# An encoder layer on one core: K and Q convolutions in a lane of their own, scan outputs kept in the keys' tile, masks in their own stream, and a reordered start

## The chip, the cores and the metric

One core of a Trainium2 chip runs the whole layer in one launch. The metric is the device time in microseconds (us); the kernel before has a median of 1962.57 us over 3 runs (1962.05 to 1963.68). PE is the matrix engine, DVE the vector engine, ACT the scalar engine, POOL the general one, SP the engine that issues nearly all DMAs.

## The reference, cut to what matters

```python
h = rmsnorm(h_res, norm1_w)                 # 16 meta tokens + 1024 tokens, 1024 channels
q, k, v, z, beta, a, sc_b, sc_c, sc_x, gate_a, gate_b = split(h @ w_in)
qkv = silu(depthwise_conv5(concat(q, k, v)))
q = l2norm(q) * 128**-0.5 ; k = l2norm(k)   # 8 heads of 128 channels
# per head, forwards and backwards, in chunks: lmat = strict(beta * (k k^T) * decay), (I + lmat)^-1, then
#   v_new = u - w S ; o = q exp(g) S + (q k^T * decay) v_new ; S = S exp(g_last) + k_dec^T v_new
o = rmsnorm(o_fwd + o_bwd) * dn_norm_w * silu(z)
merged = sigmoid(gate_a) * (o @ w_bdn) + sigmoid(gate_b) * ((sc_b * conv3(sc_c * sc_x)) @ w_bsc)
h_res += merged @ w_out ; h_res += swiglu(rmsnorm(h_res, norm2_w)) @ w_down ; out = rmsnorm(h_res)
```

## The kernel before, in words

All large products split each fp32 operand into a high and a low fp32r part and add three products (high by high, high by low, low by high); in `dense_steps` (L332) one step is these three matmuls for one of eight 128-row pieces of the weight.

**The start (L989 to L1172).** Nine row tiles `xs[t]` of the input are loaded. `root(t)` squares a tile on ACT and takes the inverse root on POOL; `scaled(t)` multiplies on DVE by the root and by `w1row`, the norm weight on all 128 partitions (one 512 KB DMA on SP, L1070); `turned(t)` transposes on PE into two PSUM banks; `highs(t)` writes the high parts `hTh` on ACT, `lows(t, g)` the low parts `al` on DVE. `keep_warm(n)` is n transposes of the identity whose result nothing reads. `gen0` and `gen1` are the generators of the first two weight units, K and Q of head 0; `u0` and `u1` are their weights, the high part cast on ACT, the low part subtracted on POOL. `rows` holds the convolution taps, which two transposes turn into `wc` and `cols`; `wba` are the 32 columns of beta and a, used by `small_gates`.

**Phase 1 (L1303 to L1325).** A Python planner writes the order of all engines by hand. It takes 128-column weight units one after another (24 units of K, Q and V, 8 of z, 24 of the short convolution, 7 of the gates; 9 gate units are left to phase 2, `LATE`), and after each dense step it calls `run_streams()` and `pump()`. Streams are generators that emit the small work of a head: `g_gates` (once), `g_decay` (the decay factors `PQ`), `g_norm` (norms and the K K^T and Q K^T products), `g_inv` (the triangular inverse) and `g_scan` (the two scans of a head and its output). `pump` fills DVE with jobs from lanes: the convolutions, the forward substitution `fs`, small `norm` jobs. Of the lanes that are ready, the one with the least weighted DVE time goes first. `T` holds the planner's clock for each engine; it sets the order only.

**The tiles in question.** `kq` (three buffers) holds a head's keys and queries, [128, 2, 1040]; `NP` and `PQ` (two buffers each) the inverse and the decayed products. The scan accumulates its outputs in `oacc`, views of `NP`; at its end they are scaled on ACT (L893), transposed on PE, multiplied by z on DVE into the other half of `NP` (L899) and stored to `o_d` (L902). `freed` counts scans that have read their `kq` for the last time, `done` scans whose store is issued. K of head h takes a `kq` buffer when `freed` is at least h - 2; its first writer is the ACT copy L389. `g_norm` of head h takes `NP` when the store of head h - 2 is expected to be over.

**Phase 2** (from L1326) is the rest of the layer with seven products for eight blocks; its code is not touched.

## Time and profile before

| what | value |
|---|---|
| median of 3 runs | 1962.57 us (1962.05 to 1963.68) |
| the profiled execution | 1961.08 us, span 1959.4 us |
| granted TensorE clock, mean | 0.999 |
| PE busy | 1941.7 us, 99% of the span, 11962 matmuls |
| DVE, ACT, POOL busy | 1468.1, 867.9, 158.4 us |
| PE idle from 0 to 30 us (the start) | 30.00 - 24.92 = 5.08 us |
| PE idle from 30 to 960 us (phase 1) | 930.00 - 926.09 = 3.91 us |
| PE idle from 960 to 1900 us | 940.00 - 938.31 = 1.69 us |

A stretch's idle time is its length less PE's busy time in it. Matmuls are pipelined and their ends are modelled, so a matmul that waits only shortly still looks busy. The profiled execution is 1.49 us under the median.

### The profile page before, as it was taken

What the parts mean: (1) busy time and instruction counts of PE and PEld (TensorE: products, weight loads), DVE (VectorE), ACT (ScalarE), POOL (GpSimd) and SP (SyncE); (2) the same over time, 40 slices, a digit from 0 to 9 for tenths busy, and PEclk for the clock granted to TensorE, in tenths of its full rate; (3) what the DMA queues carried; (4) which work ended last, traced back from release to release, by engine and by line L of the source; (5) the groups of instructions that cost most, each with busy time, mean ns of one, the idle gap of its engine ahead of it and who ended that gap; (6) DMA issues with size and microseconds to landing.
All of it is one profiled execution on the core that took longest, in us unless ns stands there. A gap on an engine that the chain in (4) does not pass through costs nothing.

```text
span 1959.4 us, 31938 instructions
## 1 busy us (share of the span) xinstructions
PE 1941.7 (99%) x11962; PEld 1704.4 (87%) x11962; DVE 1468.1 (75%) x2804; ACT 867.9 (44%) x2014; POOL 158.4 (8%) x457
## 2 busy tenths in 40 slices
PE   8999999999999999999999999999999999999998
PEld 8998899999899999998888888887888888888887
DVE  4778778788887888787358798559787887756574
ACT  5463544646455554533445545234232332324343
POOL 3012112020110202110000000000000000000001
PEclk9999999999999999999999999999999999999999
DMA  4222332323222222224386623332666644587654
GB/s 146 68 76 80 103 99 60 87 60 87 60 76 67 85 65 79 70 69 153 103 310 246 206 88 121 115 119 73 212 232 209 209 165 163 179 279 243 194 181 155
DMA packets 243136, 264.11 MB, mean 135 GB/s; under 512 B 46820, under 2 KB 166933, under 8 KB 240549
## 3 DMA queue, kind: packets, MB, share of 16 engines
q1 hardware_dynamic: 242981, 262.07, 42.1%
q8 instruction: 94, 1.54, 0.3%
q14 instruction: 61, 0.50, 0.1%
HBM read 189.58 MB, written 72.44 MB: 134 GB/s over the span
## 4 chain that ended last, share of the span: by engine, by line
PE 89%; DVE 5%; ACT 3%; issue 1%; DMA 1%; POOL 0%; SPq 0%; POOLq 0%; DVEq 0%; ACTq 0%
PE pm L332 31%; PE pm L1382 5%; PE pd L1382 4%; PE pe L1382 3%; PE pm L1656 3%; PE pm L1658 3%; PE pm L1657 2%; PE pd L1658 2%; PE pd L1656 2%; PE pd L1657 2%; PE pe L1658 2%; PE pe L1656 2%; PE pe L1657 2%; PE pm L1814 1%; PE pm L1815 1%; PE pm L1813 1%
## 5 line engine op out<-in xcount | busy, mean ns | idle before, releaser
L332 PE MATMUL pm<-hTh,wh 128*128 128x512 f32 (+4 forms) x1328 | 483.8, 365 | 0.1
L332 PE MATMUL pm<-hTh,wl 128*128 128x512 f32 (+4 forms) x1328 | 450.5, 340 | 0.0
L332 PE MATMUL pm<-al,wh 128*128 128x512 f32 (+4 forms) x1328 | 449.6, 339 | 0.5 <-DVE al L1047 0.5
L332 PEld LDWEIGHTS pm<-hTh,wl 128*128 128x128 f32 x1328 | 249.1, 188 | 15.5
L332 PEld LDWEIGHTS pm<-hTh,wh 128*128 128x128 f32 x1328 | 250.2, 189 | 13.6 <-ACT hTh L1041 0.2
L332 PEld LDWEIGHTS pm<-al,wh 128*128 128x128 f32 x1328 | 250.4, 189 | 12.9 <-DVE al L1047 0.7
L87 DVE TENSOR_TENSOR al<-raw,ring_h 128x1024 fp32r<-128x1024 f32 x73 | 88.4, 1223 | 63.6 <-ACT ring_h L86 63.2
L86 ACT CAST ring_h<-raw 128x1024 fp32r<-128x1024 f32 x73 | 76.9, 1054 | 109.7 <-PE pd L1815 35.3
L940 DVE TENSOR_TENSOR wl<-raw,wh 128x512 fp32r<-128x512 f32 x122 | 84.1, 690 | 32.0 <-ACT wh L943 27.1
L355 DVE SCALAR_TENSOR_TENSOR kq<-ra,wc,kq 128x520 f32<-128x520 f32 (+1 forms) x128 | 95.9, 749 | 2.3 <-ACT kq L389 1.2
L821 ACT ACTIVATE w<-pd,small 128x128 f32<-128x128 f32 x128 | 40.2, 365 | 124.9 <-PE pd L814 106.4
L128 POOL TENSOR_SCALAR ss<-ss 128x1 f32<-128x1 f32 x13 | 4.6, 353 | 951.1 <-ACT b L1825 603.4
L491 DVE TENSOR_TENSOR tm<-fP,fN 128x135 f32<-128x135 f32 (+23 forms) x248 | 72.1, 291 | 10.0 <-DMA fN<-nd 3.3
L495 DVE TENSOR_TENSOR fP<-fP,tm 128x135 f32<-128x135 f32 (+23 forms) x248 | 71.8, 289 | 7.3
L943 ACT CAST wh<-raw 128x512 fp32r<-128x512 f32 x122 | 74.8, 619 | 0.1
L87 DVE TENSOR_TENSOR raw<-pair,raw 128x1024 fp32r<-128x1024 f32 (+1 forms) x42 | 48.0, 1143 | 30.4 <-ACT raw L86 30.4
L86 ACT CAST raw<-pair 128x1024 fp32r<-128x1024 f32 (+1 forms) x42 | 41.7, 992 | 58.4 <-PE pd L1382 27.5
L87 DVE TENSOR_TENSOR wl<-pair,wh 128x1024 fp32r<-128x1024 f32 (+1 forms) x42 | 48.1, 1144 | 21.7 <-ACT wh L86 21.6
L86 ACT CAST wh<-pair 128x1024 fp32r<-128x1024 f32 (+1 forms) x42 | 41.7, 992 | 46.0 <-PE pd L1382 24.7
L843 DVE SCALAR_TENSOR_TENSOR S<-S,eGl,pd 128x128 f32<-128x128 f32 x104 | 31.8, 344 | 38.2 <-PE pd L831 30.8
L130 POOL TENSOR_TENSOR small<-small,minus_half 128x9 f32<-128x9 f32 x16 | 29.5, 1842 | 353.8 <-DVE small L878 264.0
L661 POOL TENSOR_TENSOR tm<-mP,mN 1x15 f32<-1x15 f32 (+7 forms) x120 | 37.3, 311 | 237.0 <-DMA mN<-ndm 228.7
(660 smaller groups left out, 4945.7 us busy)
## 6 DMA issues: line engine op xcount, KB each, us to landing
raw<-in_w_in_dram SPq DMA_DIRECT2D x64, 512.0 KB
raw<-in_w_gate_up_dram SPq DMA_DIRECT2D x44, 512.0 KB
sums<-in_w_down_dram SPq DMA_DIRECT2D x22, 512.0 KB
t_d<-sums SPq DMA_DIRECT2D x11, 1024.0 KB
raw<-s_d SPq DMA_DIRECT2D x44, 256.0 KB
raw<-t_d SPq DMA_DIRECT2D x44, 256.0 KB
act_d<-b SPq DMA_DIRECT2D x43, 256.0 KB
raw<-act_d SPq DMA_DIRECT2D x33, 256.0 KB
```

The lines of the kernel that those rows point to most:

```text
L86: nc.scalar.copy(hi, src)
L87: nc.vector.tensor_tensor(out=lo, in0=src, in1=hi.bitcast(F32), op=ALU.subtract)
L332: mm(po[:, :n], (wl if j == 2 else wh)[:, k], xl[k][:, t0:t0 + n] if j == 1 else xh[k][:, t0:t0 + n], start=(i == 0), stop=(i == 3 * KT - 1))
L355: nc.vector.scalar_tensor_tensor(out=acc, in0=raw[:, h0 + t:h0 + t + hn], scalar=wc[:, t, col:col + 1], in1=acc, op0=ALU.mult, op1=ALU.add)
L491: nc.vector.tensor_tensor(out=tv, in0=fP[:, 0:r, j:j + 1].broadcast_to([P, r, n]), in1=fN[:, j:j + 1, j + 1:32].broadcast_to([P, r, n]), o ...
L495: nc.vector.tensor_tensor(out=fP[:, 0:r, j + 1:32], in0=fP[:, 0:r, j + 1:32], in1=tv, op=ALU.subtract)
L940: nc.vector.tensor_tensor(out=u[1][1][:, k], in0=u[2][:, k], in1=u[1][0][:, k].bitcast(F32), op=ALU.subtract)
L943: nc.scalar.copy(u[1][0][:, k], u[2][:, k])
L1382: mm(bank[t], a[:, c], b, start=fresh, stop=first and k == 3 and j == 2, skip_group_check=not first)
L1656: mm(po, ah[:, k], bhk, start=k == 0, stop=False)
L1657: mm(po, ah[:, k], blk, start=False, stop=False)
L1658: mm(po, al[:, k], bhk, start=False, stop=k == 3)
```

## The change

- K and Q convolutions go into a lane `kq` with weight 0.2; V's stay in `conv`, and a ready `conv` job gives way to any other.
- At the end of a scan all eight output tiles are scaled into the keys' half of the head's `kq` (`osc`), then transposed; the product with z goes into the queries' half (`oTs`), and the store reads that. `NP` is given back once the scaling is done (`scaled`), and K of head h waits for `done` instead of `freed`.
- The masks for the meta tokens (`Dm`) leave `g_gates` and become a stream `g_meta`; `g_norm` copies the small product out raw and multiplies by mask and scale in one instruction later.
- The norm weight is loaded as one row of 4 KB from ACT's queue and spread to all partitions by two products with a row of ones (`one_row`) and two DVE copies. 44 identity transposes become 8, the two products, and 24.
- Tiles 0 to 2 are reordered: `scaled(2)` ahead of the high and low parts, the weight's split ahead of `highs(1)`, the second halves of the low parts last, and the transposes of `rows` behind the first sweep of `gen0`.

```diff
-    WEIGHT = {"conv": 1.0, "short": 1.0, "fs": 0.33, "norm": 0.1}
+    WEIGHT = {"kq": 0.2, "conv": 1.0, "short": 1.0, "fs": 0.33, "norm": 0.1}
...
+            if len(cand) > 1 and "conv" in cand:
+                cand.remove("conv")
...
-                    while freed < h - 2:
+                    while done < h - 2:
...
-                job = enqueue("conv", conv_job(raw, dst, col, sub, META if i == 1 else 0))
+                job = enqueue("conv" if i == 2 else "kq", conv_job(raw, dst, col, sub, META if i == 1 else 0))
...
-        nc.vector.tensor_tensor(out=Nm, in0=pt[:META, P:P + META], in1=Dm[:, h], op=ALU.mult)
+        nc.vector.tensor_copy(Nm, pt[:META, P:P + META])
...
-        nc.vector.tensor_scalar(out=Nm, in0=Nm, scalar1=cc[:META, 8, 0:1], scalar2=None, op0=ALU.mult)
+        while not gated:
+            yield T["pe"] + 100
+        nc.vector.scalar_tensor_tensor(out=Nm, in0=Nm, scalar=cc[:META, 8, 0:1], in1=Dm[:, h], op0=ALU.mult, op1=ALU.mult)
         on("dve", 950)
-        while done < h - 1 or "PQ" not in st_:
+        while "PQ" not in st_ or h > 1 and "scaled" not in heads[h - 2]:
             yield T["pe"] + 100
         if h > 1:
-            yield heads[h - 2]["stored"]
+            yield heads[h - 2]["scaled"]
...
+        osc, oTs = (kq[:, a, 0:SEQ].rearrange("p (c t) -> p c t", c=NC) for a in range(2))
+        t = [0, 0]
+        for c in range(NC):
+            nc.scalar.activation(osc[:, c], oacc[c], AF.Copy, scale=y[:, c:c + 1])
+            t[c // 4] = A(P)
+        st_["scaled"] = t[1]
         for c4 in range(2):
-            oT = NP[:, 4 * c4:4 * c4 + 4, 1 - c4]
+            oT = oTs[:, 4 * c4:4 * c4 + 4]
             pt = newbank()
+            yield t[c4]
             for c in range(4):
-                nc.scalar.activation(oacc[4 * c4 + c], oacc[4 * c4 + c], AF.Copy, scale=y[:, 4 * c4 + c:4 * c4 + c + 1])
-                t = A(P)
-            yield t
-            for c in range(4):
-                transpose(pt[:, c], oacc[4 * c4 + c])
+                transpose(pt[:, c], osc[:, 4 * c4 + c])
...
+        if ndec == 1 and not metas and not gated:
+            metas.append([g_meta(), T["dve"] + HOP, None])
...
+        nc.gpsimd.memset(one_row, 1.0)
+        nc.scalar.dma_start(w1row[0:1], norm1_w[0:1, :])
...
-        nc.sync.dma_start(w1row, norm1_w[0:1, :].broadcast_to([P, D]))
...
-        keep_warm(44)
+        keep_warm(8)
+        for c in (slice(0, 512), slice(512, 1024)):
+            pw = psm()
+            mm(pw, one_row, w1row[0:1, c], start=True, stop=True)
+            nc.vector.tensor_copy(w1row[:, c], pw)
+        keep_warm(24)
...
         turned(1)
         root(2)
+        scaled(2)
         highs(0)
         lows(0, 0)
-        scaled(2)
+        nc.scalar.copy(u0[1][0], u0[2])
+        nc.gpsimd.tensor_tensor(out=u0[1][1], in0=u0[2], in1=u0[1][0].bitcast(F32), op=ALU.subtract)
+        keep_warm(4)
+        turned(2)
+        highs(1)
+        lows(1, 0)
+        highs(2)
+        lows(2, 0)
         lows(0, 1)
-        highs(1)
...
         lows(1, 1)
...
         lows(2, 1)
+        root(3)
+        steps(gen0)
         pt = psd()
         transpose(pt[:, :120], rows[:120, 0], 120)
         pt2 = psd()
         transpose(pt2[:, :25], rows[:25, 1], 25)
-        root(3)
-        steps(gen0)
```

The new lines shift the later ones: L332 of before is L334 of the changed kernel, L389 is L391, L893 is L896, L902 is L909.

**First place: PE at the start.** `pm<-ident` are the identity transposes, `xr` the input tiles, `pe<-rows` the taps' transposes, `hTh` and `al` the high and low parts. Before:

```order
L83 MATMUL pm_174<-ident 128x128 x44
L83 MATMUL pd_247<-ident,xr_155 128x128 x4
L83 MATMUL pe_252<-ident,xr_155 128x128 x4
L83 MATMUL pm_174<-ident 128x128 x4
L83 MATMUL pd_266<-ident,xr_156 128x128 x4
L83 MATMUL pe_271<-ident,xr_156 128x128 x4
L83 MATMUL pm_174<-ident 128x128 x6
L83 MATMUL pd_295<-ident,xr_157 128x128 x4
L83 MATMUL pd_300<-ident,xr_157 128x128 x4
L83 MATMUL pe_314<-ident,rows 128x120
L83 MATMUL pe_316<-ident,rows 128x25
L332 MATMUL pm_321<-hTh_129,wh_194 128x336 x4
```

The changed kernel, from tile 2's transposes to the beta and a columns (ahead of it stand 8 identity transposes, the two 512-column products, 24 identity transposes and tiles 0 and 1):

```order
L83 MATMUL pd_286<-ident,xr_160 128x128 x4
L83 MATMUL pm_291<-ident,xr_160 128x128 x4
L334 MATMUL pm_311<-hTh_129,wh_196 128x336 x4
L334 MATMUL pm_311<-hTh_130,wh_196 128x336 x4
L334 MATMUL pm_311<-al_126,wh_196 128x336 x4
L334 MATMUL pm_311<-al_127,wh_196 128x336 x2
L334 MATMUL pm_311<-al_128,wh_196 128x336 x2
L334 MATMUL pm_311<-hTh_129,wl_197 128x336 x4
L334 MATMUL pm_311<-hTh_130,wl_197 128x336 x4
L83 MATMUL pe_336<-ident,rows 128x120
L83 MATMUL pe_338<-ident,rows 128x25
L1065 MATMUL pe_351<-hTh_129,wba 64x336
```

The two transposes of the taps have moved from ahead of the 24 matmuls of the sweep to behind them, directly ahead of the first matmul that needs `wba`.

**Second place: ACT at the start**, from tile 1's high parts on; `jk_first` is the squaring of a tile, `wc` and `cols` read the taps' banks. Before:

```order
L1041 CAST hTh_129<-pd_266 128x4x128
L1041 CAST hTh_130<-pe_271 128x4x128
L1100 CAST wh_194<-raw_180 128x1024
L1041 CAST hTh_129<-pd_295 128x4x128
L1041 CAST hTh_130<-pd_300 128x4x128
L1016 ACTIVATE jk_first,rs_168<-xr_158 128x1024
L1115 ACTIVATE wc<-pe_314 128x120
L1116 COPY cols<-pe_316 128x24
L1117 ACTIVATE cols<-pe_316 128x1
L1118 CAST wba<-wba_raw 128x8x32
L1121 CAST wh_196<-raw_187 128x1024
L1016 ACTIVATE jk_first,rs_169<-xr_159 128x1024
```

The changed kernel:

```order
L1114 CAST wh_196<-raw_182 128x1024
L1053 CAST hTh_129<-pd_262 128x4x128
L1053 CAST hTh_130<-pe_267 128x4x128
L1053 CAST hTh_129<-pd_286 128x4x128
L1053 CAST hTh_130<-pm_291 128x4x128
L1028 ACTIVATE jk_first,rs_171<-xr_161 128x1024
L1131 ACTIVATE wc<-pe_336 128x120
L1132 COPY cols<-pe_338 128x24
L1133 ACTIVATE cols<-pe_338 128x1
L1134 CAST wba<-wba_raw 128x8x32
L1137 CAST wh_198<-raw_189 128x1024
L1028 ACTIVATE jk_first,rs_172<-xr_162 128x1024
```

ACT's row is nearly the same, but the rows from `wc` on now read PSUM banks that PE fills only after the sweep.

**Third place: ACT where K of head 5 begins and the scan of head 2 ends.** `ra` and `kq` are the two copies of a K chunk out of PSUM, `vS` the scaled values of the next scan, `wh` weight casts, `rb` the tanh of a convolution. Before:

```order
L893 ACTIVATE NP_3502<-NP_3502,small_2619 128x128 x4
L429 COPY ra_5784<-pm_5841 128x384
L893 ACTIVATE NP_3502<-NP_3502,small_2619 128x128 x4
L943 CAST wh_5894<-raw_5708 128x512
L360 ACTIVATE rb_5941<-kq_4641 128x520
L388 COPY ra_5964<-pm_5898 128x336
L389 ACTIVATE kq_5962<-pm_5898,wc 128x336
L943 CAST wh_5894<-raw_5708 128x512
L764 ACTIVATE vS_5956<-pd_5957,small_4625 128x128 x3
L764 ACTIVATE vS_5956<-pd_5977,small_4625 128x128 x3
```

The changed kernel:

```order
L431 COPY ra_5823<-pm_5903 128x384
L896 ACTIVATE kq_1342<-NP_3401,small_2505 128x128 x8
L950 CAST wh_5963<-raw_5758 128x512 x2
L362 ACTIVATE rb_6026<-vT_4724 128x520
L390 COPY ra_6039<-pm_5967 128x336
L391 ACTIVATE kq_6037<-pm_5967,wc 128x336
L768 ACTIVATE vS_6051<-pd_6052,small_4426 128x128 x3
L768 ACTIVATE vS_6051<-pd_6062,small_4426 128x128 x3
L768 ACTIVATE vS_6051<-pd_6083,small_4426 128x128 x3
L529 ACTIVATE PQ_5930<-PQ_5930,negG_691 128x128 x2
L362 ACTIVATE rb_6106<-vT_4724 128x520
```

The scaling writes `kq_1342` of head 2 instead of `NP`, and `kq_6037` of head 5, the third buffer after it, is the same memory: its first write now follows the stores that read head 2's outputs.

25 lines of the change are left out of this document (11 added, 14 removed).

## Prediction

> **What bounds the kernel now.** I read the page first, then PE's busy time by stage, then what PE waited for, then the two places that the change touches in order of time.
>
> ```profile
> span 1959.4 us, 31938 instructions
> PE 1941.7 (99%) x11962; PEld 1704.4 (87%) x11962; DVE 1468.1 (75%) x2804; ACT 867.9 (44%) x2014; POOL 158.4 (8%) x457
> 0.00:30.00 30.00, 24.92 (x170) 22.20 (x170) 15.33 (x26) 17.41 (x34) 11.32 (x22) 1.00 0.77 237
> 30.00:960.00 930.00, 926.09 (x7359) 861.90 (x7360) 734.80 (x1872) 472.72 (x1492) 129.64 (x401) 1.00 0.28 79
> 960.00:1900.00 940.00, 938.31 (x4177) 776.15 (x4176) 686.28 (x871) 354.33 (x456) 9.29 (x17) 1.00 0.55 184
> PE pd L714 <- ACT T L708: 1.7, 1, 1.7
> ```
>
> In the stage rows PE's busy time and instruction count come first. PE is the bound everywhere. What can be had is its idle time: 30.00 - 24.92 = 5.08 us in the start, 930.00 - 926.09 = 3.91 us in phase 1, and 1.69 us up to 1900 us, where the code is unchanged. In phase 1 the largest wait is one of 1.7 us for ACT in an inverse; the others share the remaining 2.2 us. DVE and ACT have room, and scans, norms and convolutions lie beside the dense matmuls. The change takes no dense matmul away, so the question is whether it closes these few gaps or opens others.
>
> **The start.** Its rows in order of time (start, duration):
>
> ```profile
> 1.46 6.49 PE L83 MATMUL pm<-ident 128*128 128x128 f32 x44 [1.46 <-POOL ident masks.py:199]
> 1.69 0.43 SPq L1070 DMA_DIRECT2D w1row<-in_norm_w_dram  x1
> 5.57 1.06 ACT L1016 ACTIVATE jk_first<-xr 128x1024 f32<-128x1024 f32 x1 [3.28 <-DMA xr<-in_x_dram]
> 7.72 1.41 DVE L1022 SCALAR_TENSOR_TENSOR xr<-xr,rs,w1row 128x512 f32<-128x512 f32 x2 [7.72 <-POOL rs L130]
> 8.30 1.06 ACT L1016 ACTIVATE jk_first<-xr 128x1024 f32<-128x1024 f32 x1 [1.58 <-DMA xr<-in_x_dram]
> 8.53 0.65 PE L83 MATMUL pd<-ident,xr 128*128 128x128 f32 x4 [0.58 <-DVE xr L1022]
> 9.67 1.06 ACT L1016 ACTIVATE jk_first<-xr 128x1024 f32<-128x1024 f32 x1 [0.21 <-DMA xr<-in_x_dram]
> 11.19 0.59 ACT L1041 CAST hTh<-pe 128x512 fp32r<-128x512 f32 x1
> 13.10 1.05 ACT L1100 CAST wh<-raw 128x1024 fp32r<-128x1024 f32 x1
> 14.38 0.68 DVE L1047 TENSOR_TENSOR al<-pd,hTh 128x512 fp32r<-128x512 f32 x1
> 14.98 0.74 DVE L1047 TENSOR_TENSOR al<-pe,hTh 128x256 fp32r<-128x256 f32 x2
> 15.82 0.21 PE L83 MATMUL pe<-ident,rows 25*128 25x25 f32 x1 [0.97 <-DVE al L1047]
> 15.96 1.51 PE L332 MATMUL pm<-hTh,wh 128*128 128x336 f32 x8
> 16.14 0.26 ACT L1115 ACTIVATE wc<-pe 128x120 f32<-128x120 f32 x1
> 16.35 0.19 ACT L1117 ACTIVATE cols<-pe 128x1 f32<-128x1 f32 x1
> 17.03 0.41 ACT L1118 CAST wba<-wba_raw 128x256 fp32r<-128x256 f32 x1 [0.49 <-DMA wba_raw<-in_w_in_dram]
> 17.47 0.43 DVE L1119 TENSOR_TENSOR wba<-wba_raw,wba 128x256 fp32r<-128x256 f32 x1 [0.49 <-ACT wba L1118]
> 17.31 1.41 PE L332 MATMUL pm<-al,wh 128*128 128x336 f32 x8
> 17.34 1.05 ACT L1121 CAST wh<-raw 128x1024 fp32r<-128x1024 f32 x1
> 18.47 2.89 POOL L1122 TENSOR_TENSOR wl<-raw,wh 128x1024 fp32r<-128x1024 f32 x1 [0.91 <-ACT wh L1121]
> 19.81 0.32 PE L1053 MATMUL pe<-hTh,wba 128*64 128x336 f32 x1
> 22.36 1.28 DVE L1022 SCALAR_TENSOR_TENSOR xr<-xr,rs,w1row 128x1024 f32<-128x1024 f32 x1 [3.27 <-POOL rs L130]
> 29.98 0.41 PE L332 MATMUL pm<-al,wh 128*128 128x320 f32 x1 [0.46 <-DVE al L1047]
> ```
>
> The reader sees three chains here: tile by tile from the load through ACT, POOL and DVE to PE; the taps from PE through ACT (`wc`, `wba`) to small_gates on PE; and the second weight through ACT and POOL.
>
> Removed: 512 KB of w1row ahead of tiles 1 and 2 on SP's queue. From 0 to 10 us the queues moved 256 GB/s, from 10 to 20 us 349:
>
> ```profile
> 0.00:10.00 10.00, 7.95 (x55) 7.48 (x56) 1.41 (x2) 4.12 (x7) 1.94 (x12) 1.00 0.80 256
> 10.00:20.00 10.00, 7.95 (x53) 6.62 (x52) 8.14 (x15) 8.69 (x18) 6.43 (x7) 1.00 1.09 349
> ```
>
> That is 524 KB / 256 to 349 GB/s = 1.5 to 2.0 us; tile 1 lands at about 6.6 instead of 8.30, tile 2 at 7.9 instead of 9.67. Tile 0 stood ahead of w1row; I leave it at 5.57.
>
> Added: two products of 512 columns in fp32 and two DVE copies. The nearest product, of 256 columns, takes at most 0.484 us from its start to its modelled end:
>
> ```profile
> L583 PE MATMUL pe<-kq x128: 377/379/484, 110.3 to 815.0; 128*128 128x256 f32 x128
> ```
>
> So a product of 512 columns lies between four 128-column transposes (0.106 us each, 0.207 while PE is slow, both below: 0.42 or 0.83) and twice 0.484 = 0.97. I take 0.83, since it falls where PE is slow. When the 4 KB row lands the trace does not show: issued near 0.8 us, it is there by 5.1 at the latest if it takes as long as tile 0's 512 KB (issued from 0.8 on, read at 5.57), which would put turned(0) 0.9 us later; I take 3.2, since it is a hundredth of that. 8 transposes end near 3.2, the products near 5.0, the copies (0.68 each, as the low parts' row) near 5.7: earlier than tile 0's root at 7.7, so the spreading is hidden behind tile 0's load, at no cost; without that cover it would cost its 2.5 us. The 24 transposes end at 7.6 to 8.4, and turned(0) starts at 8.53 as before. Then, by the same durations and 2.15 us from a squaring's start to DVE's (5.57 to 7.72): root(1) 6.8 to 8.1, scaled(1) 9.1 to 10.5, root(2) 8.1 to 9.3, scaled(2) 10.5 to 11.95 (12.39 to 13.8 before), turned(2) 11.7 to 13.0. ACT: highs(0) to 10.5, the weight's cast to 11.55, highs(1) to 12.7, highs(2) to 13.9. The sweep starts at 13.4 instead of 15.96, a gain of 2.6 us, the 0.97 us wait for a bank included.
>
> It is given back at three places. DVE: lows(0,0), (1,0) to 13.3, lows(2,0) to 14.0, then three times 0.74 to 16.25, so the sweep's last two low-part matmuls wait, and with two of these and eight more at 0.156 us (16 matmuls from 17.31 to 19.81) PE is through at 17.9, only 1.9 us early. PE: the transposes of the taps stand behind it, 17.9 to 18.35. ACT: wc, cols and wba stand behind those, and small_gates behind wba: 18.4 + 0.4 (wc to the end of cols, 16.14 to 16.54) + 0.41 + 0.43 and about 0.1 of hand-overs = 19.8. Before: 19.81. Behind wba on ACT stands the second weight's cast, 1.9 us later than before (19.2 against 17.34), then on POOL its low part (2.89, to 23.2, when small_gates and tile 3's transposes, 3.2 us on PE, are just done) and root(4), which makes scaled(4) 1.8 us later than its 22.36. DVE had stood idle for 3.27 us ahead of it, and its next steps wait for PE and ACT, so of this delay about 1 us reaches scaled(5) and less than 0.1 us tile 5's low part, for which PE waits at 29.98. Sum of the start: +0.1 us. Bounds: -2.6 (nothing given back) and +2.0 (tiles 1 and 2 land no earlier, by up to 2.0 us, and the chain through the taps still lies behind).
>
> The clock in these rows: the first 14 identity transposes take 2.90 / 14 = 0.207 us each, the later ones 3.30 / 31 = 0.106, though the granted clock reads 1.00 in both stretches:
>
> ```profile
> 1.50:4.40 2.90, 2.90 (x14) 1.00 0.79 206
> 4.60:7.90 3.30, 3.30 (x31) 1.00 0.98 353
> ```
>
> PE speeds up at about 4.5 us, 3 us after its first matmul. If a wait for the row of weights behind the 8 transposes starts that anew, the 24 transposes take 0.207 each too: 1.46 + 8 x 0.207 + 2 x 0.83 + 24 x 0.207 = 9.75 instead of 8.53 for turned(0), and its own eight transposes cost another 0.8 us: +2.0 us. [...]
>
> **Phase 1.** PE's instructions are the same, in 7 more interruptions of the dense rows (350 against 343). The matmul behind an interruption, always a high-part one, runs longer:
>
> ```profile
> L332 PE MATMUL pm<-hTh,wh 128*128 128x384 f32 x320 | 115.9, 362 | 0.1
> L332 PE MATMUL pm<-al,wh 128*128 128x384 f32 x320 | 107.6, 336 | 0.0
> ```
>
> That is 115.9 - 107.6 = 8.3 us over 320 steps of this width, which is a third of the steps' time, so some 25 us over 343 interruptions, under 0.1 us each. But two short interruptions cost no less in themselves than one long; I take 0, bound 7 x 0.1 = +0.7. Eight DVE instructions less: DVE is not the bound, 0. Masks' stream: the same DMA and instructions beside head 0's decay, 0, without cover one DMA wait. Scaling into kq: the same 64 ACT rows and 16 DVE rows, 0. New V convolution order: V is needed only by the scan, which waits for the inverse; 0 while that holds. NP is returned earlier, so inverses and scans start earlier, but PE's end is set by its own work: 0.
>
> The new wait: K of head h copies into kq on ACT (L389) only after head h - 3's stores have read that buffer. For head 5 both fall together; in the trace of before, at the same place:
>
> ```profile
> 472.24 0.55 ACT L389 ACTIVATE kq<-pm,wc 128x336 f32<-128x336 f32 x1
> 473.06 0.36 SPq L902 DMA_DIRECT2D o_d<-NP  x1
> SPq L676 <- DMA pd<-fP: 32.7, 8, 6.1
> 472.00:479.00 7.00, 6.74 (x28) 1.00 0.29 78
> ```
>
> The last store is issued 0.82 us after ACT would write. The nearest row for a store's landing is L676's wait, 32.7 / 8 = 4.1 us in the mean, 6.1 at most. So ACT stands for 0.8 + 4.1 = 4.9 us (0.8 to 6.9). [...] Behind it on ACT queue nine scalings of the next scan, the masks' exponentials, copies out of PSUM and the next weight's casts, by the last row about 7 us of work (6.74 of 7.00 us busy before). PE's order then has 72 dense matmuls of 320, 384 and 322 columns (at 0.156 us for 336 and in proportion 11.5 us) and small ones, about 2 us, before the first matmul that needs ACT (the next inverse): 13.5 - 7 - 2 (DVE's transposes) = 4.5 us of cover against 4.9. I take 0, as the 0.4 between them is less than either side is known to; bounds 0 and +2.9 (6.9, the cover partly used). Heads 4, 6 and 7 have 6.9, 5.2 and 6.8 us of PE work between the last transposes and the first K chunk's end, against 1.4 (an estimate: a multiply of 0.75 us on DVE as its low parts' row, 0.36 for the issue, hand-overs) + 4.1 = 5.5 us: 0 to 0.3 us on ACT, nothing on PE; head 3 has 17.
>
> **Sum:** +0.1 on the profiled execution (1961.08, span 1959.4 and 1.7 around it), so 1961.2 there; the median of the runs stands 1.49 higher, so 1962.57 + 0.1 = 1962.7.
>
> **Rivals.** *Faster:* the earlier norms and inverses take away PE's phase-1 waits: -3.91 if all go, and -2.6 if the start keeps its gain: 1956.1. For it: each is a wait for a stream's late result. Against it: they are chance meetings in a fixed order (1.7 us the largest), which a new order replaces by others. *Slower:* the stores hold ACT in front of K's copies. It decides from a landing of 5.5 us on: at 6.1 head 5 costs 6.9 - 4.5 = 2.4, head 6 1.4 + 6.1 - 5.2 = 2.3, heads 4 and 7 0.6 and 0.7: +6.0 if PE feels each, 1968.6. Against it: 6.1 is the longest of a chain of small pieces, and ACT has 44% load. *The clock starts anew:* +2.0, 1964.7; against it, the products keep PE busy. *The start does not gain at all* is what I forecast.
>
> **Chances.** Forecast 0.59; clock 0.07, also inside 0.2% (3.9 us, about what a measurement here can tell from no change); faster by over 0.2% 0.19; slower 0.15. The range runs from 1957.5 (most of phase 1's waits, or half of them and the start's gain) to 1967.5 (the stores at most places); the likeliest case's own is 1960.0 to 1965.6.
>
> **What would show it.** Right: the first 336-column matmul near 13.4 us, small_gates near 19.8, PE idle in 30 to 960 us between 2 and 7 us, an ACT wait for a DMA before head 5's L391. Wrong: small_gates under 18 us; PE waits in phase 1 under 1 us or over 8; identity transposes at 0.2 us after 6 us.

## The result and the profile after

The changed kernel takes 1982.57 us (median; 1982.03 to 1983.78), the kernel before in the same series 1962.31 (1961.89 to 1963.68). The ratio is 1.0104, 95% interval 1.0092 to 1.0117: slower by 20.3 us. The forecast was 1962.7 with a range up to 1967.5, so it was wrong.

First the same rows as of before: the page's span and engine totals, the three stages (us, then busy time and count of PE, PEld, DVE, ACT, POOL, then the granted clock, the DMA share and GB/s), PE's waits (total, times, longest), ACT's two waits at K's copy.

```profile
span 1980.8 us, 31932 instructions
PE 1950.1 (98%) x11952; PEld 1708.9 (86%) x11952; DVE 1467.6 (74%) x2806; ACT 866.5 (44%) x2014; POOL 166.8 (8%) x458
```

```profile
0.00:30.00 30.00, 26.40 (x150) 21.92 (x150) 14.96 (x24) 15.65 (x31) 13.61 (x23) 1.00 0.72 219
30.00:960.00 930.00, 911.56 (x7264) 848.48 (x7265) 729.74 (x1864) 468.03 (x1481) 135.86 (x401) 0.99 0.27 77
960.00:1900.00 940.00, 938.36 (x4186) 776.64 (x4185) 676.01 (x861) 349.41 (x457) 9.24 (x17) 1.00 0.55 183
```

```profile
PE pe L585 <- DVE PQ L621: 11.2, 8, 5.3
PE pe L83 <- ACT jk L547: 4.3, 2, 3.6
...
ACT kq L391 <- DMA o_d<-kq: 6.5, 2, 5.7
ACT kq L391 <- issue: 3.1, 1, 3.1
```

The loss is in phase 1: PE's idle time from 30 to 960 us is 18.44 us, before 3.91, and 95 PE instructions fewer fit into the stretch. Up to 1900 us PE idles 1.64 us, before 1.69: phase 2 is unchanged. The largest wait has a new name, L585: the eight products of K with K and Q in each head's norm (`kkq`, L583 before). They have two PSUM banks of the kind `pe`, so the third product waits until DVE has read the first (L617, L621), and DVE needs the exponentials of ACT (L529).

The largest of these waits in order of time, on ACT, DVE and PE:

```profile
480.58 0.42 ACT L390 COPY ra<-pm 128x336 f32<-128x336 f32 x1
486.64 0.54 ACT L391 ACTIVATE kq<-pm,wc 128x336 f32<-128x336 f32 x1 [5.65 <-DMA o_d<-kq]
487.08 2.42 ACT L768 ACTIVATE vS<-pd,small 128x128 f32<-128x128 f32 x9
489.33 0.75 ACT L529 ACTIVATE PQ<-PQ,negG 128x128 f32<-128x128 f32 x2
...
489.82 0.64 DVE L617 SCALAR_TENSOR_TENSOR NP<-pe,small,PQ 128x128 f32<-128x128 f32 x2 [3.35 <-ACT PQ L529]
492.11 0.42 DVE L621 TENSOR_TENSOR PQ<-pe,PQ 128x256 f32<-128x256 f32 x1
...
492.68 1.19 PE L585 MATMUL pe<-kq 128*128 128x256 f32 x2 [5.25 <-DVE PQ L621]
```

Head 5's first K copy stands 5.65 us for the stores out of its buffer; behind it on ACT stand nine scalings and then the exponentials of head 4's norm; behind those DVE; behind DVE the third product on PE. PE stood 5.25 us. Behind each of the three longest stalls (5.25, 3.62 and 2.65 us) the granted clock reads 0.50 (a stretch with the first stall, then the stretches behind the three):

```profile
488.00:492.40 4.40, 0.00 (x0) 0.00 (x0) 1.60 (x4) 4.35 (x15) 0.00 (x0) 1.00 0.49 124
492.50:495.80 3.30, 3.12 (x9) 2.97 (x10) 3.20 (x8) 1.38 (x4) 0.00 (x0) 0.50 0.00 0
...
649.50:652.70 3.20, 3.20 (x14) 3.10 (x15) 1.16 (x4) 1.58 (x9) 0.00 (x0) 0.50 0.02 5
700.70:704.00 3.30, 3.30 (x12) 3.30 (x11) 3.17 (x8) 1.20 (x4) 0.00 (x0) 0.50 0.00 1
```

It reads 0.50 for some 3.4 us behind each of the three, so by estimate each costs another 1.7 us or so (half of 3.4). The stall at 646 us has another source, a piece on DVE:

```profile
641.97 0.48 DVE L408 TENSOR_SCALAR rb<-ra,cols 128x512 f32<-128x512 f32 x1
642.49 1.54 DVE L413 SCALAR_TENSOR_TENSOR rb<-ra,cols,rb 128x512 f32<-128x512 f32 x2
643.94 0.48 DVE L408 TENSOR_SCALAR rb<-ra,cols 128x512 f32<-128x512 f32 x1
644.46 1.54 DVE L413 SCALAR_TENSOR_TENSOR rb<-ra,cols,rb 128x512 f32<-128x512 f32 x2
647.03 0.28 DVE L871 TENSOR_TENSOR NP<-pd,NP 128x128 f32<-128x128 f32 x1
...
647.35 0.37 ACT L865 ACTIVATE NP<-pd,eG 128x128 f32<-128x128 f32 x1 [4.25 <-DVE NP L871]
...
649.50 0.90 PE L83 MATMUL pe<-ident,kq 128*128 128x128 f32 x3 [3.62 <-ACT jk L547]
```

A whole short convolution runs there without a break. The planner had let it wait until its result was due and then forced it (`force`). A scan's step (L871) waits behind it on DVE, ACT (L865) for that step, and a norm's transposes on PE for ACT.

The start, on PE:

```profile
1.59 1.97 PE L83 MATMUL pm<-ident 128*128 128x128 f32 x8 [1.59 <-POOL ident masks.py:199]
3.48 3.78 PE L1100 MATMUL pm<-w1row,one_row 1*128 1x512 f32 x4
7.19 4.73 PE L83 MATMUL pm<-ident 128*128 128x128 f32 x24
11.76 0.60 PE L83 MATMUL pd<-ident,xr 128*128 128x128 f32 x4
15.93 1.52 PE L334 MATMUL pm<-hTh,wh 128*128 128x336 f32 x8 [0.51 <-ACT hTh L1053]
20.31 0.43 PE L83 MATMUL pe<-ident,rows 120*128 120x120 f32 x2
21.83 0.37 PE L1065 MATMUL pe<-hTh,wba 128*64 128x336 f32 x1 [1.09 <-DVE wba L1135]
```

and two stretches of the same:

```profile
7.30:11.00 3.70, 3.70 (x18) 1.00 1.11 348
11.20:12.40 1.20, 1.20 (x13) 1.00 1.05 341
```

The two products stand as four matmuls (x4) of together 3.78 us. From 7.3 to 11.0 a transpose takes about 3.70 / 18 = 0.206 us; the twelve from 11.76 to 13.07 take (13.07 - 11.76) / 12 = 0.109 each: PE is slow until about 11.1. small_gates starts at 21.83, before at 19.81.

### The profile page after: what moved, and what is told of

Its sections match the earlier page's. It is cut to its first block, busy times and chain, and to the rows that moved or that the text cites. A ratio compares the mean times of both kernels' runs of the same rounds, so it can differ in the third digit from the quotient of the medians.

```text
span 1980.8 us, 31932 instructions
## 1 busy us (share of the span) xinstructions
PE 1950.1 (98%) x11952; PEld 1708.9 (86%) x11952; DVE 1467.6 (74%) x2806; ACT 866.5 (44%) x2014; POOL 166.8 (8%) x458
## 4 chain that ended last, share of the span: by engine, by line
PE 90%; DVE 5%; ACT 2%; DMA 1%; issue 1%; POOL 0%; SPq 0%; POOLq 0%; ACTq 0%; DVEq 0%
PE pm L334 31%; PE pm L1402 5%; PE pd L1402 4%; PE pe L1402 3%; PE pm L1676 2%; PE pm L1678 2%; PE pm L1677 2%; PE pd L1677 2%; PE pd L1678 2%; PE pd L1676 2%; PE pe L1678 2%; PE pe L1677 2%; PE pe L1676 2%; PE pm L1834 1%; PE pm L1835 1%; PE pm L1833 1%
## 5 line engine op out<-in xcount | busy, mean ns | idle before, releaser
L334 PE MATMUL pm<-hTh,wh 128*128 128x512 f32 (+4 forms) x1328 | 487.3, 368 | 0.6 <-ACT hTh L1053 0.5
L334 PE MATMUL pm<-al,wh 128*128 128x512 f32 (+4 forms) x1328 | 451.2, 340 | 0.6 <-DVE al L1059 0.6
L334 PE MATMUL pm<-hTh,wl 128*128 128x512 f32 (+4 forms) x1328 | 451.7, 341 | 0.0
L334 PEld LDWEIGHTS pm<-hTh,wl 128*128 128x128 f32 x1328 | 250.2, 189 | 15.7
L334 PEld LDWEIGHTS pm<-hTh,wh 128*128 128x128 f32 x1328 | 251.4, 189 | 14.3 <-ACT hTh L1053 1.1
L334 PEld LDWEIGHTS pm<-al,wh 128*128 128x128 f32 x1328 | 251.7, 190 | 13.2 <-DVE al L1059 1.1
L87 DVE TENSOR_TENSOR wl<-pair,wh 128x1024 fp32r<-128x1024 f32 (+1 forms) x42 | 48.0, 1144 | 21.5 <-ACT wh L86 21.4
L390 ACT COPY ra<-pm 128x320 f32<-128x320 f32 (+3 forms) x72 | 32.3, 449 | 58.5 <-PE pm L334 58.3
```

The costliest lines, as they stand in the source:

```text
L87: nc.vector.tensor_tensor(out=lo, in0=src, in1=hi.bitcast(F32), op=ALU.subtract)
L334: mm(po[:, :n], (wl if j == 2 else wh)[:, k], xl[k][:, t0:t0 + n] if j == 1 else xh[k][:, t0:t0 + n], start=(i == 0), stop=(i == 3 * KT - 1))
```

## The experiments

Two theories stood at the outset: the stores hold ACT in front of K's copies (store theory), or the new queue (lane) delays other DVE work (lane theory). The rival to both was that any other order of the same work loses about as much (reshuffle theory). Five series were run; the kernel before had medians of 1962.05, 1961.97, 1962.01, 1962.09 and 1962.61 us in them, and each difference below is to that of its own series, each bracket the 95% interval of the ratio.

### Parts undone and parts alone

The changed kernel with the outputs back in NP:

```
-        osc, oTs = (kq[:, a, 0:SEQ]... for a in range(2))
+            oT = NP[:, 4 * c4:4 * c4 + 4, 1 - c4]      # `freed` and `stored` as before
```

> The changed kernel, but the outputs stay in NP as before (scaled in place, stored from NP; K of head h waits in the planner for `freed`, norms for `stored`). Store theory: the three PE stalls behind head 5's, 6's and 7's first K copy (5.25, 1.27 and 2.65 us) and two slow-clock stretches after them (1.7 us each) go: 1982.6 - 12.6 = 1970.0, between 1968 and 1972, and no ACT wait for o_d at L391. Lane theory (the new queue for K and Q starves the short convolutions, which then come in one forced piece): the forced piece stays, so no more than 2 us are won: 1980 to 1983. Reshuffle theory (any other order has as many chance waits): somewhere in 1975 to 1990, with PE waits of other kinds.

Measured 1981.49, +19.4 us [1.0083 to 1.0113]. No copy of K waits for a store any more, and almost nothing is won: PE stands at the same products.

```profile
PE pe L585 <- DVE PQ L621: 9.1, 7, 3.3
```

The price that the store theory gave (1968 to 1972) fails here; a forced piece stays, at 739 us now, as the lane theory said. But the stores are not out of it. On DVE the first writings into NP (L617) now wait 1.23, 3.11 and 3.83 us, and NP is what the stores of the head two before it read. The store and the second longest of these waits:

```profile
675.15 2.52 SPq L906 DMA_DIRECT2D o_d<-NP  x1
683.81 0.61 DVE L617 SCALAR_TENSOR_TENSOR NP<-pe,small,PQ 128x128 f32<-128x128 f32 x2 [3.11 <-DMA NP<-pd]
```

The view names another DMA that moved at the same time, but L617 also waits for this store's semaphore, whose last update comes at 683.73. The other two waits, to 386.08 and 791.07, end within 0.15 us of the last update of such a store too. The two later stores landed 8.6 and 8.5 us after their issue, where the planner reckons 4 (`STORE`), and PE's two longest waits at these products (3.27 and 3.25 us) stand behind them. So this edit moved the store wait from K's copy to the norm.

The changed kernel with K's copies ordered later:

```
-                    while done < h - 2:
+                    while done < h - 2 or h > 2 and T["pe"] < heads[h - 3]["stored"] + 3000:
```

> The changed kernel, outputs in the keys' place; only the planner asks that K of head h takes its buffer at least 7 us after the end of scan h-3 in its own reckoning (before: 0.9 us for head 5, 4.7 and 6.2 for heads 6 and 7), so ACT's copy stands behind other work of the streams in ACT's order. Store theory: the same 12.6 us are won as with the outputs in NP: 1968 to 1973, which says that it is the meeting of copy and store and not the place. Lane theory: 1979 to 1983. Reshuffle theory: 1975 to 1990.

Measured 1984.36, +22.3 [1.0100 to 1.0130]. ACT waits no more than 0.2 us for o_d, yet:

```profile
PE pe L585 <- DVE PQ L621: 12.0, 9, 4.6
```

L617 waits for no DMA here either, so the wait at L585 doesn't need the stores. Before the longest (4.62 us, to 583.75) ACT has this order:

```profile
578.45 2.44 ACT L768 ACTIVATE vS<-pd,small 128x128 f32<-128x128 f32 x9 [3.21 <-issue]
580.72 1.32 ACT L529 ACTIVATE PQ<-PQ,negG 128x128 f32<-128x128 f32 x4
```

The nine scalings of V stand ahead of the norm's exponentials, and PE's transposes of V for them started only at 578.15, after a wait of 1.06 us for the scan's output product on DVE (L906). Then L617 stands behind three pieces of V's convolution, until 582.07. The place of these products says how they came there. Start of a head's first such product minus the issue of the last store of the head two before it, heads 2 to 7, from the rows of L585 (L583) and of the store in each trace: before 5.6, 23.2, 26.8, 18.5, 24.1, 21.5 us; changed kernel -1.5, 6.8, -2.5, -1.4, -3.6, -1.6. For head 4 the rows are these, first of before (its store at 473.06 stands in the prediction), then of the changed kernel:

```profile
499.88 0.59 PE L583 MATMUL pe<-kq 128*128 128x256 f32 x2
```

```profile
479.81 0.81 PE L585 MATMUL pe<-kq 128*128 128x256 f32 x3
481.03 1.58 SPq L909 DMA_DIRECT2D o_d<-kq  x2
```

The new queue finishes K and Q earlier, and `scaled` in place of `stored` lets the norm go at once; so its products meet the end of a scan for all of these heads but head 3, where DVE and ACT have scalings, V's convolution, output products and weight parts to do.

The kernel before with the outputs in the keys' place alone:

```
-            oT = NP[:, 4 * c4:4 * c4 + 4, 1 - c4]
+            oT = oTs[:, 4 * c4:4 * c4 + 4]             # osc, oTs in kq; `done` and `scaled`
```

> The kernel before with one part alone: outputs scaled into and stored from the keys' buffer. In the planner's reckoning heads 5, 6 and 7 then take their buffer 0.46 us after the end of the scan three heads earlier, head 4 3.0 us after. Store theory: three stalls of the size seen at 487 us (5.25 + 1.7 of slow clock) and about half of one: 1962.3 + 20.9 + 2.5 = 1985.7, between 1978 and 1988. Lane theory: there is no K/Q queue, so 1962 to 1966. Reshuffle theory: 1965 to 1980.

Measured 1984.90, +22.9 [1.0101 to 1.0135]: the store theory's number. The norm's products lie 23.7 us or more behind the stores from head 3 on, and PE waits for `Nm`, the first thing a norm makes, behind K's copies:

```profile
ACT kq L389 <- DMA o_d<-kq: 21.9, 4, 7.9
PE pe L83 <- DVE Nm L566: 17.8, 4, 6.5
```

So each of the two meetings, copy with store and norm with scan, can cost without the other. (How much of the second is due to the norm's place and how much to the order around it was not parted.)

The changed kernel with one queue for all convolutions:

```
-                job = enqueue("conv" if i == 2 else "kq", conv_job(...))
+                job = enqueue("conv", conv_job(...))      # no "kq" lane, no cand.remove("conv")
```

> The changed kernel with all convolutions in one queue as before. In the planner's reckoning heads 5, 6 and 7 take their buffer 4.7, 10 and 7.3 us after the end of the scan three heads earlier (changed kernel: 0.9, 4.7, 6.2). Store theory: of the 12.6 us some 1 to 2 stay, so 1971 to 1973; lane theory in its pure form: the forced piece at 645 us goes with its slow clock, 3.6 + 1.7 = 5.3: 1977.3; both: about 1966. Against the lane theory speaks that the planner still forces 68 steps here (62 in the changed kernel, 36 in the one before): if forced steps cost by their number, nothing is won there.

Measured 1970.43, +8.4 [1.0027 to 1.0057]: 12 us less than the changed kernel, just under the 1971 to 1973 of the store theory. But the norm's products are 25.9 us or more behind the stores again from head 3 on, and no copy of K waits for a store, so this edit removes both meetings. Forced steps (DVE pieces that the planner has to push through when a buffer or a result is due) are 68 here against 62 in the changed kernel, so their number is not what makes the 20 us.

The queue, the start and the masks' stream alone, and the changed kernel with its norms later:

```
-            yield heads[h - 2]["scaled"]
+            yield heads[h - 2]["scaled"] + 20000
```

> The kernel before with one part alone: K's and Q's convolutions in a queue of their own ahead of V's and the short ones; outputs stay in NP. Lane theory, in the form that the first runs suggest (the new queue finishes K and Q so early that the norm's products of head h meet the end of scan h-2, some 20 us earlier than before; there DVE and ACT are full and PE stands at these products): the products begin within 8 us of the last store of scan h-2, PE waits 6 to 12 us for PQ, and with one to three slow-clock stretches of 1.7 us the time is 1962.3 + 8 to 16 = 1970 to 1978. Store theory: no copy waits for a store here, so 1962 to 1965.

> The changed kernel, but the planner lets the norm's products of head h start no earlier than 20 us after scan h-2 is scaled; queue for K and Q, outputs in the keys' place and the rest stay. Lane theory in the form above: the waits for PQ (11.2 us) shrink to under 2, their two slow-clock stretches go (3.4), and the copies of K fall at other places too (in the planner's reckoning 9.7, 10.6 and 7.3 us after the end of the scan, not 0.9, 4.7 and 6.2); forced steps fall from 62 to 37, so the 3.6 us wait at 645 us with its 1.7 goes as well: 1982.6 - 9.2 - 3.4 - 5.3 = 1964.7, between 1963 and 1969. If the meeting of norm and scan is not the cause: 1976 to 1985.

> The kernel before with the new start alone. What the trace of the changed kernel shows (small_gates 2.0 us later, dense matmul 100 2.1 us later) is the whole effect: 1962.3 + 2.1 = 1964.4, between 1963.5 and 1965.5, the plan of phase 1 being that of before. Rival: phase 1 takes the delay up: 1962 to 1963.

> The kernel before with the masks' stream alone (head masks made by a stream of their own, Nm multiplied later). It does no other work and adds no wait for PE, but it moves the plan: the planner forces 72 steps (36 before). If the masks' stream costs nothing and forced steps cost nothing by their number: 1962 to 1964. If forced steps cost (the piece at 645 us in the changed kernel: 3.6 + 1.7 us): 1966 to 1975.

The queue alone: 1966.05, +4.1 [1.0008 to 1.0027], between the store theory's 1965 and the lane theory's 1970, so neither had it. Its products lie 1.4 to 5.9 us behind the stores, but PE waits only 1.9 us for PQ, so nearness is not enough. In the run with the outputs back in NP they lay as near (1.6 to 7.3 us), and there PE waited 9.1 us, as two stores landed late; here DVE's first writing into NP waits for no DMA. The norms later: 1968.16, +6.2 [1.0018 to 1.0038], 14 us less than the changed kernel, within the expected range; products 17.4 to 20.3 us behind, and

```profile
PE pe L585 <- DVE PQ L621: 1.2, 4, 0.5
```

This one edit also moved K's copies away from the stores (ACT waits 0.2 us for o_d in all), so it mends both meetings and does not part them. The start alone: 1964.06, +2.1 [1.0003 to 1.0021], as read from the trace. The masks' stream alone: 1967.58, +5.6 [1.0017 to 1.0036], without a single wait on PE in phase 1 of over 1.4 us. PE's idle time from 30 to 960 us is 930.00 - 922.93 = 7.07 us there, before 3.91, and the mean granted clock is 0.998, before 0.999; no wait names the masks, so it looks like the cost of another order.

### The terms in the changed kernel's own order

To price a wait without moving the plan, the stores got another source (the outputs' values are left out), and then one forced piece lost its work too:

```
-            nc.sync.dma_start(o_d[h][...], oT)
+            nc.sync.dma_start(o_d[h][...], high_tiles[0][:, :, C0 + META:C0 + META + P].bitcast(F32))
...
+                if j != 3:                               # second kernel, in short_job
                     nc.vector.scalar_tensor_tensor(out=yc[:, :512], ...)
```

> The changed kernel with every engine's order as it is; only the store's source differs: it writes 512 columns of a constant tile instead of the outputs (so the outputs' values are left out), and K's copies wait for no store, only for DVE's last write into the buffer. That prices the store wait in the changed kernel's own order. At 481 us ACT then stands about 1 us instead of 5.65. Store theory: PE's waits at 487, 589 and 696 us (5.25, 1.27, 2.65) all but go, with two slow-clock stretches (3.4): 1982.6 - 12.6 = 1970, between 1969 and 1973. Norm-meets-scan theory (the norm's products stand in the tail of the scan two heads earlier, where DVE and ACT are full anyway): of each wait a part stays, as in the run where the copies were ordered later (3.99 and 4.62 us): 1977 to 1982.

> The changed kernel in its own order once more, stores from a constant tile as before (1973.1 us), and besides the four tap products of 1.54 us a pair that the planner forces into one piece on DVE at 642 us (short convolution 3) are not issued: 3.1 us of DVE work less at that one place, the output's values left out. Forced-piece theory: PE's wait of 3.6 us there and its slow-clock stretch (1.7) go: 1973.1 - 5.3 = 1967.8 (1967 to 1969.5). Rival: PE waits there for something else (the norm's squaring, ACT): 1972 to 1974.

Without the store wait: 1973.07 (1.0056 [1.0043 to 1.0070]; four executions from 1970.06 to 1975.18), 9.5 us less than the changed kernel, or 9.2 with each against its own series. ACT stands 1.30 us, PE's 5.25 becomes 1.81, and the waits of 1.27 and 2.65 us fall under 0.4:

```profile
482.63 0.54 ACT L391 ACTIVATE kq<-pm,wc 128x336 f32<-128x336 f32 x1 [1.30 <-DVE kq L906]
```

```profile
PE pe L585 <- DVE PQ L621: 4.2, 7, 1.8
```

Without the forced piece as well: 1969.21 (1.0035 [1.0022 to 1.0049]), another 3.9 us, less than the 5.3 forecast but within its range; PE's wait of 3.6 us is gone (`PE pe L83 <- ACT jk L548` totals 1.2). So in this order 9.5 us belong to the store wait, 3.9 to the forced piece, 2.1 to the start; of the 20.3 some 5 stay. PE still waits 4.2 us at the norm's products there. The longest of these waits is 1.8 us in both runs; in the run without the store wait the granted clock behind it reads 0.85, 0.50 and 0.77 in the stretches from 489.4 to 491, to 493 and to 495 us, which is some 3.4 us at 0.50. What holds it is the new queue's own work: on DVE a piece of head 5's K convolution stands ahead of L621 and waits for K's second copy (0.99 us in the run without the store wait). That is read from the trace and was not tried by itself.

### The order itself

```
-    HOP, TOPE, DEP = 200, 370, 127
+    HOP, TOPE, DEP = 210, 370, 127      # others: DEP 132; TOPE 380; of the changed kernel HOP 210, DEP 132
```

> The kernel before with one number of the planner changed: the hand-over that it reckons between engines is 210 ns instead of 200. Nothing else differs; it only gives another order of the same instructions (54 forced steps instead of 36, another place for each stream). Reshuffle theory (the order of before is a lucky one among its neighbours, and any change of the plan costs): +3 to +8 us, 1965 to 1970, like the run with the masks' stream alone (1967.6) and the one with the queue alone (1966.1). If neighbours are as good: 1962 +- 1.5.

> The kernel before with another number of the planner changed: 132 ns instead of 127 for a dependent DVE step. 30 forced steps (before: 36), other places for the streams. Reshuffle theory: +2 to +6 (1964 to 1968), as with the first such number (+3.7). If the number of forced steps decides: 1962 or below.

> The kernel before with a third number changed: 380 ns instead of 370 for the way from another engine back to PE. 51 forced steps. Reshuffle theory: +2 to +6 (1964 to 1968); if neighbours of the plan are as good as the plan itself: 1961 to 1963.

> The changed kernel with the planner's hand-over at 210 ns instead of 200, as in the first neighbour of the kernel before. In the planner's reckoning heads 5, 6 and 7 take their buffer 0, 4.7 and 6.2 us after the end of the scan three heads earlier (changed kernel: 0.9, 4.7, 6.2). If the meeting of K's copy with the stores belongs to the change and not to one unlucky order: 1981 to 1986. Reshuffle theory (the changed kernel met an unlucky order): 1965 to 1976.

> The changed kernel with 132 ns instead of 127 for a dependent DVE step, as in the second neighbour of the kernel before, which lost nothing. In the planner's reckoning heads 5, 6 and 7 take their buffer 0.9, 1.3 and 3.7 us after the scan's end, so by the store theory head 6 and 7 now stand as long as head 5 does: 1982.6 + 3 to 8 = 1985 to 1991. Reshuffle theory: 1965 to 1976.

The kernel before, planned with numbers that differ by 5 to 10 ns: 1965.67 (+3.7 [1.0010 to 1.0029]), 1960.72 (-1.4 [0.9985 to 1.0004]) and 1963.15 (+1.1 [0.9999 to 1.0017]). So among these three neighbours an order alone is worth between about -1 and +4 us; reshuffling as such can explain the 4.1 of the queue alone and most of the masks' 5.6, but not 20. The plans of the kernel before and of the masks' run with 30, 36, 51, 54 and 72 forced steps took 1960.7, 1962.1, 1963.2, 1965.7 and 1967.6 us, so the number of forced steps may be part of what makes an order worse; the queue alone does not fit this (38 in its plan, 1966.1), and no run parted it from the rest. The changed kernel with two of these numbers: 1977.94 (+15.3 [1.0066 to 1.0099]) and 1991.20 (+28.6 [1.0131 to 1.0161]). It loses in all three orders tried, but they lie 13 us apart, so the prices above hold for the one order in which they were taken. The second is where the plan put two more heads' copies 1.3 and 3.7 us after a scan, and it shows them:

```profile
ACT kq L391 <- DMA o_d<-kq: 12.8, 3, 5.3
PE pe L585 <- DVE PQ L621: 15.7, 9, 4.7
```

The first, expected between 1981 and 1986, came out lower: heads 6 and 7 cost PE 0.44 and 0.38 us at these products, and only head 5 still cost 4.7.

### The start

```
-        keep_warm(8)
+        keep_warm(20)
...
-        keep_warm(24)
+        keep_warm(12)
...
-        steps(gen0)                       # second and third: the taps within the chunk
+        steps(gen0, 5)                    # third: 3 steps ahead, and the first weight's
+        (the taps' two transposes)        # cast and POOL part behind highs(1)
+        steps(gen0, KT - 5)
```

> The kernel before with the new start alone, but 20 identity transposes stand ahead of the two products of one row and 12 behind (8 and 24 in the change). Clock theory: one-row products leave PE's clock low, 20 transposes raise it first (at about 4.5 us as before the change); the four passes then take about 1.9 us instead of 3.8, turned(0) starts at 8.5 to 9.2 instead of 11.76, the first dense matmul at 13.4 to 14.0 instead of 15.93, small_gates at 19.8 to 20.0 instead of 21.8, and the time is that of before, 1962.3 (1961.8 to 1962.8). Rival: the products' position does not matter (the row's landing or DVE's copies hold the start): 1964.

> As the run before (20 and 12 transposes around the products), and the taps' two transposes stand within the first dense chunk, after 15 of its 24 matmuls, so that the chain over wc, cols and wba runs beside its last nine. If that chain is what gives the start's gain back: small_gates at 18.0 to 18.4 instead of 19.8, and 1962.3 - 1.6 = 1960.7 (1960.0 to 1961.5), below the kernel before. If something else holds small_gates or what follows (the second weight's POOL part): 1962 to 1963.

> As the start with 20 and 12 transposes and the taps within the first chunk, but ACT's cast of the first weight stands behind tile 1's high parts, so that POOL's low part of it begins near 14 us, when DVE is through with scaling tile 2. Port theory (DVE's scaling, with both inputs in SBUF, and POOL's subtraction exclude each other: in the two runs before, POOL began at 12.05 and held DVE's 0.75 us piece for 2.91): scaling of tile 2 takes 1.4 again, the first dense matmul starts at 14.4 to 14.8 instead of 16.8, small_gates at 18.9 to 19.5, and the time is 1961.0 to 1962.0. Rival: the same clash elsewhere (POOL now holds another DVE piece): 1963 to 1965.

Measured 1965.06 (+3.1 [1.0005 to 1.0023]), 1964.01 (+2.0 [1.0000 to 1.0017]) and 1962.50 (+0.4 [0.9995 to 1.0013]; one of its eleven executions took 2406.54, the others 1961.41 to 1965.61). The first two missed, and the third came out 0.5 us above its range. The clock part was right in the first one's trace:

```profile
1.59 3.75 PE L83 MATMUL pm<-ident 128*128 128x128 f32 x20 [1.59 <-POOL ident masks.py:199]
5.27 1.98 PE L1091 MATMUL pm<-w1row,one_row 1*128 1x512 f32 x4
...
8.69 0.66 PE L83 MATMUL pd<-ident,xr 128*128 128x128 f32 x4
14.61 1.11 PE L83 MATMUL pd<-ident,xr 128*128 128x128 f32 x4 [2.27 <-DVE xr L1025]
```

Products 1.98 us, tile 0 turned at 8.69 instead of 11.76. But tile 2 came late, because of two instructions that started together (second kernel):

```profile
12.04 2.91 DVE L1025 SCALAR_TENSOR_TENSOR xr<-xr,rs,w1row 128x512 f32<-128x512 f32 x1 [0.46 <-POOL rs L130]
12.05 2.35 POOL L1106 TENSOR_TENSOR wl<-raw,wh 128x1024 fp32r<-128x1024 f32 x1
```

DVE's piece, 0.75 us elsewhere, took 2.91: as long as POOL's and some 0.55 more, though it was on record as started 0.01 us earlier. The traces of before and of the changed kernel show it from POOL's side: the second weight's part took 2.89 us, started beside a DVE scaling (18.47 behind 17.81, 22.34 behind 21.70), the first weight's 2.37 and 2.38 beside low parts, which read one input from PSUM and took 0.68 and 0.69 as elsewhere. In the first two kernels PE's wait of 2.27 us for tile 2 was followed by a slow stretch: tile 2's first four transposes took 1.11 and 1.10 us (0.60 in the changed kernel), and the granted clock from 0 to 30 us reads 0.94 in both, 1.00 in the changed kernel. That is (1 - 0.94) x 30 = 1.8 us or so by estimate. With POOL's part later, six of DVE's pieces take 4.06 us together, and the time is that of before within what the runs can tell; but in that profiled execution, itself 2.2 us above the median, the transposes ran slow longer still (four took 1.06 us at 13.22 and 0.60 at 14.68), so the gain of up to 1 us that was expected is not shown.

## Why the prediction was wrong

**The start, forecast +0.1, measured +2.1.** The failed term is the products: 2 x 0.83 us by scaling from a 256-column product, against 3.78 measured, in four matmuls. With them went the clock: after 1.97 us of transposes and the products PE stayed slow to 11.1 us, so the 24 transposes took 4.73 us, not the 2.6 to 3.4 forecast. turned(0) stood at 11.76 instead of 8.53, the sweep at 15.93 instead of 13.4. The rival "the clock starts anew" had this size (+2.0, chance 0.07) but not the reason: PE had no gap between the transposes and the products. The part on the taps was right: sweep, taps, wc, wba, small_gates follow each other as worked out, the taps' transposes stand behind the sweep at 20.31, and 1.5 us on small_gates begins (forecast: 17.9, then 1.9 us). The sweep simply began where it had begun before.

**The store wait, forecast 0 (bounds 0 and +2.9), priced at 9.5 in place.** ACT's wait was right: 4.9 forecast, 5.65 measured. The step that failed is the cover: "before the first matmul that needs ACT (the next inverse)". The first that needs ACT is the third L585 product, which needs a bank, that needs DVE, that needs ACT's exponentials behind the copy. PE had work for 487.4 - 481.0 = 6.4 us, but the exponentials only ended at 489.33 + 0.75 = 490.1, and L621 came at 492.11, as a piece of head 5's K convolution stood ahead of it on DVE (at 491.44, after 0.97 us for that K's second copy). Behind ACT's 5.65 us the queue mattered (2.42 us of scalings, then 0.75), and I had asked which PE instruction reads ACT's results, not which waits through DVE. Heads 6 and 7, forecast "0 to 0.3 us on ACT, nothing on PE", cost PE 1.27 and 2.65. There the landing was mis-sized as well: 4.1 us was taken, 6.1 at most, from other stores, but the last store ahead of head 7's copy landed 7.55 us after its issue, by its semaphore's last update, and ACT stood 3.11 us; in the trace of before these stores themselves land 2.3 to 7.9 us after their issue. The rival that the stores hold ACT was the right mechanism with too low a price (+6.0).

**The queue, forecast 0.** "0 while that holds" looked at V and the scan. What it left out is what becomes early: the norm's products moved, for five heads of six, from 5.6 to 26.8 us behind a scan's last store to 1.4 to 3.6 us ahead of it; and what becomes late: a short convolution, forced in one piece (3.9 us). "NP is returned earlier, so inverses and scans start earlier, but PE's end is set by its own work: 0" fails with it: early products stood where ACT and DVE had the end of a scan to do, and PE waited 12.0 us there even in the run whose copies hardly waited for a store. How much of the 20.3 us is due to that stays open: with the store wait taken out of the changed kernel's own order, no more than the 5 us that stay can be, while the 9.5 took both, as the store wait reached PE through these products.

**The slow clock behind a stall** stood in no term: three stretches of 3.41 us at 0.50, about 1.7 us each by estimate. **The masks** do no costly work, as forecast, but alone they cost +5.6, by another order as it seems. **The bound +0.7 for the order** was too narrow: the three neighbours of the plan differ by -1.4 to +3.7. **Phase 2** and the equal instruction counts came out as told, and "PE waits in phase 1 over 8 us" was the sign that it was wrong.

## What to carry to other kernels

When a wait is put into an engine's row of work, follow every consumer of what queues behind it, through the other engines and through PSUM banks, to the first matmul; cover counts up to that one (here 5.65 us on ACT became 5.25 on PE). Work that becomes ready earlier is no gift when PE is full anyway: look at what else those engines do at the new moment. Where a planner sets the order, time two or three neighbours of the plan before a difference of a few microseconds is put down to an edit.

## What was not expected of the hardware

**Stalls of PE and its clock.** In the changed kernel's phase 1 the clock's records show PE at 0.50 three times, for 3.41 us each, from 492.4, 649.4 and 700.6 us on; the stalls of 5.25, 3.62 and 2.65 us ended at 492.68, 649.50 and 699.57. In the run without the store wait one stretch is about twice as long: the granted clock reads 0.85, 0.50 and 0.51 from 641 to 645.5, to 649 and to 651 us, which is some 6.8 us at 0.50. How long a stall was did not decide alone. In the changed kernel the clock stayed at 1.00 behind stalls of 2.22 us (to 241.08) and 1.27 us (to 590.97), and one of 2.65 us had half the clock behind it. A stall of 1.67 us had it too, in the run with the start alone (the stretch with the stall, then the one behind it):

```profile
493.00:495.10 2.10, 0.43 (x6) 0.10 (x4) 1.03 (x2) 2.10 (x6) 0.03 (x1) 1.00 0.00 0
495.60:498.80 3.20, 3.20 (x82) 3.16 (x64) 3.06 (x5) 3.10 (x14) 0.00 (x0) 0.60 0.59 164
```

The 0.60 over 3.20 us is some 2.6 us at 0.50. A stall of 2.45 us in the first neighbour of the kernel before (to 712.88) had 1.00 behind it, from 713 to 717 us. What parts these stalls is not shown.

**Products of one row at the start.** In the changed kernel PE had no gap from 1.59 us on, yet the transposes took about 0.206 us each until 11.1, 3.9 us behind the products' end; in the trace of before they took 0.207 us each up to 4.4 us and 0.106 from 4.6 on. In the profiled execution of the last start it was the same as in the changed kernel: 20 transposes in 4.53 us, then products of 3.78 us, then transposes at 2.50 / 13 = 0.19 us, and slow ones to about 14.4. With the same twenty transposes ahead, the products took 1.98 us in the other two starts, so the start varies by itself.
